# Weights times v in a sliding-window attention: four matmuls of 512 columns become six of 256, and GpSimd takes the filler's low parts

## The chip, the cores and the metric

The kernel runs on one core of a Trainium2 chip. The core has a matrix engine (TensorE, PE in the profile, with its weight loads as PEld), VectorE (DVE), ScalarE (ACT), GpSimd (POOL), a queue that issues transfers (SyncE, SP), and 16 DMA engines between HBM and the on-chip memory SBUF. [...] The metric is the device time of one execution in microseconds.

## The reference

One decoder layer at batch 1, 1,024 positions and width 1,024, in fp32. A normalised input goes through one projection to q, k, v, gates and a recurrent branch. The part that the change touches is the attention: 16 heads of 64 in four groups that share a k and a v head, a window of 128 positions, blocks of 128 queries, and a learned sink a head:

```python
diff = qi + BLOCK - kj
band = (diff >= 0) & (diff < WINDOW)          # WINDOW = BLOCK = 128
...
m = jnp.maximum(jnp.max(s, axis=-1, keepdims=True), sink)
p = jnp.exp(s - m)
denom = jnp.sum(p, axis=-1, keepdims=True) + jnp.exp(sink - m)
o = jnp.einsum('bnkgqs,bnskd->bnqkgd', p / denom, vb)
```

A query sees exactly 128 keys: those of its own block up to itself, and of the block before those behind its own offset. The attention output is gated, projected, and merged with the recurrent branch, which is projected too. An output projection, a residual and a final normalisation end the layer.

## The kernel before

Precision is kept by splitting: an operand becomes a rounded part and the rest, and a product takes three matmuls (high by high, high by low, low by high). The kernel has three large stages: the input projection with the recurrent branch, the attention with the recurrent branch's output projection as filler between its matmuls, and the closing projections. The order of every engine's queue is the order in which the program issues instructions: it is written out by hand.

Attention runs over 32 units, eight blocks for each of four groups; a unit holds four heads by 128 queries. Because exactly 128 keys count, the weights of a unit are folded into one 128 by 128 tile a head: key slot s holds the own block's key where s is at most the query's offset, else the key of the block before. So the output is the sum over all slots of the weight times v of the block before, and over the slots up to the query's offset of the weight times the difference of the two blocks of v. For each unit:

- `scores` (L1330): eight matmuls of 256 columns into the only score buffer; `maxima_a` copies the own block to `p` on ScalarE (L1339), `maxima_d` overwrites it by mask with the block before (L1345) and takes maxima (L1350) on VectorE. `sink` writes the sink's column of `p` on GpSimd (L1318).
- `weights_a`, `weights_d`: exponentials on ScalarE (L1355), division on VectorE (L1362).
- `transposed` (L1369) puts keys on the partitions; `split_a` (L1374, ScalarE) and `split_d` (L1380, VectorE) make the high part `phc` and the low part `plc`; `masks` (L1389, GpSimd) makes masked copies `phm` and `plm`.
- `values` (L1403): four matmuls of 512 columns, `phc` and `plc` by the block before, `phm` and `plm` by the difference. The first block of a group has the two unmasked ones alone. The stationary operand holds v's high part in columns 0 to 63 and its low part in 64 to 127.
- `join_a` (L1412, L1413) and `join_d` (L1423, L1424) add the two halves of the result; `a_prep` multiplies by the gate (L1538) and splits again (L1543, L1548, L1553).

In pass u of the main loop stand the scores of unit u, the weights of u - 1, the transposes and masks of u - 2 and the values of u - 3, with pieces of filler of 12 matmuls (L173). Filler operands are cast on ScalarE (L105, list `later_a`, at the end of a pass) and their rest is subtracted on VectorE (L111, list `later_d`, early in the next pass).

`v_prep` computes per group, in the projection stage, the differences and splits of v and stores both in HBM (`vd_d`). `load_v` brings, for two units at a time, the block before and the difference to `vd`, from GpSimd's queue. Steps of the projection stage are placed by a planner that adds the costs written beside them.

The tiles of attention lie in SBUF in a stack from high to low addresses: `kq1`, `yo`, `pp`, `at`, opened by `open_attn`, in space that the recurrent branch has just left. A tile waits for whatever last used its bytes. The last block of the recurrent branch is stored from `it` and `av` by GpSimd's queue (`yl_d<-it`, `yh_d<-av`). In `pp` lie three tiles `p`, of 2,064 B a partition.

Of the kernel before, what the change touches and what calls it, by code (L numbers as in the profile page):

```python
# [22 lines left out]
P = 128  # L23
# [25 lines left out]
KEEP_BUSY = 4  # L49
SLACK = 1.0, 1.3, -1.0  # L50
BANKS = (0, 1, 2, 3), (4, 5, 6, 7)


@with_exitstack
def tile_hybrid_block(ctx, tc, x, pk, rows, posr, posi, c_row, w_ss, w_gate, w_main, w_v,
# [8 lines left out]
    def f32(ap):  # L64
        return ap.bitcast(F32)
# [40 lines left out]
        else:  # L106
            A.activation(dst[0][:], src, AF.Copy, scale=scale)

    def rest(dst, src, scale=1.0):
        if scale == 1.0:  # L110
            V.tensor_tensor(out=dst[1][:], in0=src, in1=f32(dst[0][:]), op=ALU.subtract)  # L111
# [18 lines left out]
    vd_d = [tc.dram_tile([P, 8, 2, P], F32, name=f"vd_d{g}") for g in range(NG)]  # L130
# [1023 lines left out]
    def v_prep(g):  # L1154
        t = {}
        vpp = W["vpp"]

        def f0():
            t["v"] = vpp.tile([P, 8, 64], F32, tag="v32", name="v32")
            dma(t["v"][:], v_d[:, :, g, :], G)  # L1160

        def f1():
            t["d"] = vpp.tile([P, 8, 64], F32, tag="d32", name="d32")
            V.tensor_tensor(out=t["d"][:, 1:8, :], in0=t["v"][:, 1:8, :],
                            in1=t["v"][:, 0:7, :], op=ALU.subtract)
            V.tensor_copy(t["d"][:, 0, :], t["v"][:, 0, :])

        def f2():
            for n_ in ("vs", "dv"):
                t[n_] = vpp.tile([P, 8, P], F32R, tag=n_, name=n_)  # L1170
            A.copy(t["vs"][:, :, 0:64], t["v"][:])
            A.copy(t["dv"][:, :, 0:64], t["d"][:])

        def f3():
            for n_, d_ in (("v", "vs"), ("d", "dv")):
                V.tensor_tensor(out=t[d_][:, :, 64:128], in0=t[n_][:],
                                in1=f32(t[d_][:, :, 0:64]), op=ALU.subtract)
            dma(vd_d[g][:, 1:8, 1, :], t["vs"][:, 0:7, :], G)
            dma(vd_d[g][:, :, 0, :], t["dv"][:], G)

        waiting[1].extend([[("S", 0, 0, f0)], slots(6), [("D", 0, 0.85, f1)],
                           [("A", 1.24, 0, f2)], [("D", 0, 1.38, f3)]])


# [109 lines left out]
    def load_kq(m):
        g, t0 = m // 4, (m % 4) * 256
# [6 lines left out]
        dma(qs[:], q_d[g][m % 4].rearrange("(a j) t -> a j t", j=4))  # L1302
        U["kq", m] = ks, qs

    def load_v(m):
        g, n0 = m // 4, (m % 4) * 2
        vd = at.tile([P, 2, 2, P], F32R, tag="vd", name="vd", bufs=2)
        if n0:
            dma(vd[:], vd_d[g][:, n0:n0 + 2, :, :], G)
        else:  # L1310
            dma(vd[:, 0, 0, :], vd_d[g][:, 0, 0, :], G)
            dma(vd[:, 1, :, :], vd_d[g][:, 1, :, :], G)
        U["v", m] = vd

    def sink(u):
        px = U["p", u] = W["pp"].tile([P, 4, P + 1], F32, tag="p", name="p")
# [47 lines left out]

    def transposed(u):
        px = U.pop(("s", u))[1]
        pt = psx.tile([P, 4, P], F32, tag="t", name="pt")
        for j in range(4):
            W["pe"] = T.transpose(pt[:, j, :], px[:, j, 0:P], ident[:])  # L1369
        U["t", u] = [pt]  # L1370

    def split_a(u):
        phc = at.tile([P, 4, P], F32R, tag="phc", name="phc")
        A.copy(phc[:], U["t", u][0][:])  # L1374
        U["t", u].append(phc)

    def split_d(u):
        pt, phc = U.pop(("t", u))
        plc = at.tile([P, 4, P], F32R, tag="plc", name="plc")
        V.tensor_tensor(out=plc[:], in0=pt[:], in1=f32(phc[:]), op=ALU.subtract)  # L1380
        U["m", u] = phc, plc

    def masks(u):
        phc, plc = U["m", u]
        ms = []
        if u % 8:
            for s_, tag in ((phc, "phm"), (plc, "plm")):
                d_ = W["yo"].tile([P, 4, P], F32R, tag=tag, name=tag)
                G.affine_select(out=d_[:], in_=f32(s_[:]), pattern=[[0, 4], [1, P]],  # L1389
                                compare_op=ALU.is_ge, fill=0.0, base=0,  # L1390
                                channel_multiplier=-1)
                ms.append(d_)
        U["m", u] = [phc, plc], ms

    def values(u):
        n = u % 8
        vd = U["v", u // 2]
        full, masked = U.pop(("m", u))
        prods = [(vd[:, n % 2, 1 if n else 0, :], m) for m in full]
        prods += [(vd[:, n % 2, 0, :], m) for m in masked]  # L1400
        pv = psx.tile([P, 4 * P], F32, tag="v", name="pv")
        for i, (b, m) in enumerate(prods):
            W["pe"] = T.matmul(pv[:], b, m[:].rearrange("p j q -> p (j q)"),  # L1403
                               start=(i == 0), stop=(i == len(prods) - 1))
        U["pv", u] = [pv[:].rearrange("p (a e q) -> p a e q", a=2, e=2)]
        if n % 2 == 0 and u // 2 + 1 < 16:
            load_v(u // 2 + 1)

    def join_a(u):
        pvv = U["pv", u][0]  # L1410
        ob = W["yo"].tile([P, 2, P], F32, tag="ob", name="ob")
        A.copy(ob[0:64], pvv[64:128, :, 0, :])  # L1412
        A.copy(ob[64:128], pvv[0:64, :, 1, :])  # L1413
        U["pv", u].append(ob)

    def join_d(u):
        g, n = u // 8, u % 8
        pvv, ob = U.pop(("pv", u))
        if n % 2 == 0:
            W["yq"] = W["yo"].tile([P, 2, 256], F32, tag="yq", name="yq", bufs=3)  # L1420
            U["yq", u // 2] = W["yq"]
        yo = W["yq"][:, :, (n % 2) * P:(n % 2 + 1) * P]
        V.tensor_tensor(out=yo[0:64], in0=pvv[0:64, :, 0, :], in1=ob[0:64], op=ALU.add)  # L1423
        V.tensor_tensor(out=yo[64:128], in0=pvv[64:128, :, 1, :], in1=ob[64:128], op=ALU.add)  # L1424


    ps_ctx = ExitStack()
# [9 lines left out]
    def prep_r(e, i):  # L1437
        def f1():
            O[e, i] = slot()
            cast(O[e, i], R[e][i])  # L1440
        later_a.append(f1)
        later_d.append(lambda: rest(O[e, i], R[e][i]))
        if "att" not in W:
            do_later()

# [248 lines left out]
    for u in range(32 + 3):  # L1694
# [4 lines left out]
            maxima_d(u)  # L1699
        if 1 <= u < 33:  # L1700
            weights_a(u - 1)
        do_later(later_d)
        low = [steps_[2] for steps_ in high]
        while high:
            high.pop(0)[1]()
# [21 lines left out]
        if "hpool" in W:  # L1727
            for f in low:
                f()
            if late and ("gq", late[0]) in U and u >= loaded[late[0]] + 2:  # L1730
                high.append(a_prep(late.pop(0)))
                high[0][0]()
        do_later(later_a)
        if u >= 3 and u % 2 == 0:
            late.append((u - 3) // 2)
        if u >= 2 and len(loaded) < 16 and len(loaded) <= (u - 2) // 2 and (
# [323 lines left out]
```

## Time and profile before

| what | value |
|---|---|
| median of 3 runs | 907.06 us (906.17 to 907.93) |
| the profiled execution's own time | 907.17 us |
| its span, first to last instruction | 905.5 us |
| PE, DVE, ACT, POOL busy | 99%, 79%, 63%, 14% of the span |
| granted TensorE clock | 0.999 |
| HBM traffic | 199 GB/s over the span |

A row of a timeline gives start and duration in us, engine, line, operation, written tile and read tiles, shape and count; in square brackets the idle time before it and what ended it. A row of a group ends with busy us and mean ns of one, then the idle time before. A stage row gives for each engine the busy time and, in parentheses, the number of instructions. A row of waits gives the total in us, the times and the longest.

### The profile page before, as it was taken

The numbers are of one execution on the slowest core, as the hardware profiler recorded it, in microseconds if no ns is written. First come the engines' busy times: TensorE is split into PE (matmuls) and PEld (weight loads), VectorE is DVE, ScalarE is ACT, GpSimd is POOL, SyncE is SP. The second block draws the span as 40 slices with busy tenths as digits, with TensorE's granted clock in tenths as the row PEclk, the third lists the DMA queues.
The fourth block names the chain that finished last, engine by engine and source line by source line (L and its number), as shares of the span: only waits on it lengthen the run. The fifth ranks groups of instructions, "written<-read, shape, count | busy, mean of one in ns | idle before, by whom it ended". The sixth has DMA issues, their size and how long they took to land.

```text
span 905.5 us, 12654 instructions
## 1 busy us (share of the span) xinstructions
PE 895.4 (99%) x4258; PEld 746.2 (82%) x4259; DVE 717.1 (79%) x1073; ACT 567.4 (63%) x1098; POOL 124.7 (14%) x216
## 2 busy tenths in 40 slices
PE   9999999999999999999999999999999999999997
PEld 6789888888888888888888888888888888888886
DVE  6987688988669875987788597999989846578855
ACT  7965554654566855786485884888888732115535
POOL 6520251200000000000000002343443300000000
PEclk9999999999999999999999999999999999999999
DMA  9829489772435353354446367996655289416604
GB/s 355 339 69 286 164 258 319 256 235 95 151 128 180 123 209 135 125 183 162 157 144 213 105 201 242 344 401 217 214 202 203 83 306 367 140 47 232 209 1 186
DMA packets 87349, 180.74 MB, mean 200 GB/s; under 512 B 8642, under 2 KB 29138, under 8 KB 87284
## 3 DMA queue, kind: packets, MB, share of 16 engines
q1 hardware_dynamic: 83200, 167.07, 52.5%
q0 software_dynamic: 3936, 12.59, 4.4%
q8 instruction: 34, 0.56, 0.3%
q14 instruction: 31, 0.25, 0.1%
q10 hardware_dynamic: 148, 0.27, 0.1%
HBM read 121.34 MB, written 58.95 MB: 199 GB/s over the span
## 4 chain that ended last, share of the span: by engine, by line
PE 52%; issue 42%; DVE 3%; ACT 2%; DMA 1%; POOL 0%; DVEq 0%; ACTq 0%; POOLq 0%
PE rp L173 14%; PE bk L709 10%; PE out L1863 6%; PE pmain L173 5%; PE s_ps L1330 3%; PE pv L1403 3%; PE pmain L485 2%; PE bk L485 2%; PE pt L1369 1%; DMA yl_d<-it 1%; PE pmain L1579 1%; PE pmain L1580 1%; PE pmain L1578 1%; ACT jk L1881 1%; PE bk L256 1%
## 5 line engine op out<-in xcount | busy, mean ns | idle before, releaser
L709 PE MATMUL bk<-nh,wh 128*128 128x512 f32 x368 | 143.4, 390 | 0.0
L709 PE MATMUL bk<-nl,wh 128*128 128x512 f32 x368 | 143.3, 389 | 0.0
L709 PE MATMUL bk<-nh,wl 128*128 128x512 f32 x368 | 98.4, 389 | 0.0
L111 DVE TENSOR_TENSOR wl<-r,wh 128x512 fp32r<-128x512 f32 x109 | 74.8, 692 | 23.3 <-ACT wh L105 23.2
L105 ACT CAST wh<-r 128x512 fp32r<-128x512 f32 x107 | 65.6, 618 | 32.1 <-PE rp L173 11.8
L709 PEld LDWEIGHTS bk<-nh,wl 128*128 128x128 f32 x368 | 69.1, 188 | 14.3
L709 PEld LDWEIGHTS bk<-nh,wh 128*128 128x128 f32 x368 | 69.2, 188 | 14.2
L709 PEld LDWEIGHTS bk<-nl,wh 128*128 128x128 f32 x368 | 69.1, 188 | 14.1
L709 PE MATMUL bk<-hh,wh 128*128 128x512 f32 x184 | 71.7, 390 | 0.0
L709 PE MATMUL bk<-hl,wh 128*128 128x512 f32 x184 | 71.6, 389 | 0.0
L111 DVE TENSOR_TENSOR wl<-ws,wh 128x512 fp32r<-128x512 f32 x76 | 52.1, 686 | 7.2 <-ACT wh L105 7.1
L62 POOL DMA_DIRECT2D yh_d<-av x1 | 0.6, 567 | 371.9 <-ACT av L1092 371.9
L1355 ACT ACTIVATE p<-p,small 128x129 f32<-128x129 f32 x128 | 50.0, 396 | 0.0
L709 PE MATMUL bk<-hh,wl 128*128 128x512 f32 x184 | 49.2, 389 | 0.0
L105 ACT CAST wh<-ws 128x512 fp32r<-128x512 f32 x76 | 46.0, 614 | 4.8 <-DVE ws L731 2.4
L709 PEld LDWEIGHTS bk<-hh,wl 128*128 128x128 f32 x184 | 34.6, 188 | 7.1
L709 PEld LDWEIGHTS bk<-hh,wh 128*128 128x128 f32 x184 | 34.6, 188 | 7.1
L709 PEld LDWEIGHTS bk<-hl,wh 128*128 128x128 f32 x184 | 34.6, 188 | 7.1
L1330 PEld LDWEIGHTS s_ps<-ks,qs 128*128 128x128 f32 x256 | 34.1, 189 | 4.4 <-DVE p L1345 2.0
L1330 PE MATMUL s_ps<-ks,qs 128*128 128x256 f32 (+1 forms) x256 | 35.6, 282 | 0.3 <-DVE p L1345 0.2
L709 PE MATMUL bk<-hha,wh 128*128 128x512 f32 x92 | 35.8, 390 | 0.0
L709 PE MATMUL bk<-hla,wh 128*128 128x512 f32 x92 | 35.8, 389 | 0.0
(378 smaller groups left out, 2293.1 us busy)
## 6 DMA issues: line engine op xcount, KB each, us to landing
r<-w_main SPq DMA_DIRECT2D x100, 256.0 KB, 4.2
wada<-w_ss SPq DMA_DIRECT2D x16, 512.0 KB, 9.0
qs<-q_d SPq DMA_DIRECT2D x16, 512.0 KB, 5.2
wo_d<-wr SPq DMA_DIRECT2D x28, 256.0 KB, 3.1
wo<-wo_d SPq DMA_DIRECT2D x14, 512.0 KB, 5.6
ks<-k_d SPq DMA_DIRECT2D x12, 384.0 KB, 4.3
xt<-x SPq DMA_DIRECT2D x8, 512.0 KB, 7.1
sma_d<-c SPq DMA_DIRECT2D x16, 256.0 KB, 4.4
```

The lines of the kernel that those rows point to most:

```text
L105: A.copy(dst[0][:], src)
L111: V.tensor_tensor(out=dst[1][:], in0=src, in1=f32(dst[0][:]), op=ALU.subtract)
L173: mm = T.matmul(ps[hf], ww, xx[kc][hf], start=(kc == 0 and ww is w_h and xx is xh), stop=(kc == KC - 1 and xx is xl))
L256: T.matmul(bk[i % 2], zero[:, 0:P], zero, start=True, stop=True)
L485: T.matmul(starts[c][hf], ww[:, c0:c0 + P], xh[kc][hf], start=(kc == 0 and t_ == "h"), stop=(kc == KC - 1 and t_ == "l"))
L709: W["pe"] = T.matmul(ps, ww[:, kc * P:(kc + 1) * P], b[kc][i], start=(first and n == 0), stop=(n == 11), skip_group_check=not first)
L1330: W["pe"] = T.matmul(o, qs[:, j, qc], ks[:, kb:n % 2 + 2, b, :], start=(b == 0), stop=(b == 1))
L1355: A.activation(px[:, j, :], px[:, j, :], AF.Exp, bias=sm[:, 0, j:j + 1], accum_out=sm[:, 1, j:j + 1])
L1369: W["pe"] = T.transpose(pt[:, j, :], px[:, j, 0:P], ident[:])
L1403: W["pe"] = T.matmul(pv[:], b, m[:].rearrange("p j q -> p (j q)"), start=(i == 0), stop=(i == len(prods) - 1))
L1578: T.matmul(o, hh[kc][th][:, ts_], wh[:, cols], start=(kc == 0), stop=False)
L1863: T.matmul(o, a[k][x_][:, p * P:(p + 1) * P], b[k][y_][:, cols], start=(first and k == 0 and i == 0), stop=(k == 3 and i == 2), skip_group ...
```

## The change

Queries of a unit are taken in two halves. For the first 64 queries of a block the base is v of the block before, as it was; the difference, own less before, matters only for keys 0 to 63, since all later keys are of the block before. For the last 64 the base is v of the own block, and the correction, before less own, matters only for keys 64 to 127. So a correction has 64 keys, and its high and low weights are stacked on 128 partitions: per half two base matmuls and one for the correction, each of 256 columns. A block of v is loaded once, as `vb`, and serves two units; the signed differences come in pairs of units, repeated on both halves of the partitions. The masks become four selects of 64 partitions by 256 columns into one tile `pm`. Of the filler's subtractions those issued in attention go to GpSimd, behind their cast at the end of the pass.

```diff
+TOP, END = slice(0, 64), slice(64, 128)
...
-    def rest(dst, src, scale=1.0):
+    def rest(dst, src, scale=1.0, eng=V):
         if scale == 1.0:
-            V.tensor_tensor(out=dst[1][:], in0=src, in1=f32(dst[0][:]), op=ALU.subtract)
+            eng.tensor_tensor(out=dst[1][:], in0=src, in1=f32(dst[0][:]), op=ALU.subtract)
...
         def f1():
-            V.tensor_tensor(out=t["d"][:, 1:8, :], in0=t["v"][:, 1:8, :],
-                            in1=t["v"][:, 0:7, :], op=ALU.subtract)
+            for h, a, b in ((TOP, 1, 0), (END, 0, 1)):
+                V.tensor_tensor(out=t["d"][h, 1:8, :], in0=t["v"][h, a:a + 7, :],
+                                in1=t["v"][h, b:b + 7, :], op=ALU.subtract)
...
-            dma(vd_d[g][:, 1:8, 1, :], t["vs"][:, 0:7, :], G)
-            dma(vd_d[g][:, :, 0, :], t["dv"][:], G)
-        waiting[1].extend([[("S", 0, 0, f0)], slots(6), [("D", 0, 0.85, f1)],
+            dma(vs_d[g], t["vs"][:], G)
+            for l, half_ in enumerate((TOP, END)):
+                dma(dv_d[g][:, :, l, :], t["dv"][half_, :, :], G)
+        waiting[1].extend([[("S", 0, 0, f0)], slots(6), [("D", 0, 1.4, f1)],
...
         load_v(0)
+        load_d(0)
+        load_v(1)
...
+    def load_v(u):
+        vb = U["v", u] = at.tile([P, P], F32R, tag="vb", name="vb", bufs=4)
+        dma(vb[:], vs_d[u // 8][:, u % 8, :], G)
+
+    def load_d(m):
+        n0 = m % 4 * 2
+        vd = U["d", m] = at.tile([P, 2, 2, P], F32R, tag="vd", name="vd", bufs=2)
+        dma(vd[:], dv_d[m // 4][:, n0:n0 + 2, :, :].unsqueeze(0).to_broadcast([2, 64, 2, 2, P]), G)
...
-        pt = psx.tile([P, 4, P], F32, tag="t", name="pt")
+        pt = psx.tile([P, 2, 4, 64], F32, tag="t", name="pt")
...
     def masks(u):
         phc, plc = U["m", u]
-        ms = []
         if u % 8:
-            for s_, tag in ((phc, "phm"), (plc, "plm")):
-                d_ = W["yo"].tile([P, 4, P], F32R, tag=tag, name=tag)
-                G.affine_select(out=d_[:], in_=f32(s_[:]), pattern=[[0, 4], [1, P]],
-                                compare_op=ALU.is_ge, fill=0.0, base=0,
-                                channel_multiplier=-1)
+            pm = W["yo"].tile([P, HALF], F32R, tag="pm", name="pm")
+            lo, hi = slice(0, 256), slice(256, HALF)
+            for to, s_, from_, cols in ((TOP, phc, TOP, lo), (END, phc, END, hi),
+                                        (END, plc, TOP, lo), (TOP, plc, END, hi)):
+                d = 1 if cols is lo else -1
+                G.affine_select(out=pm[to, cols], in_=f32(s_[from_, cols]),
+                                pattern=[[0, 4], [d, 64]], compare_op=ALU.is_ge, fill=0.0,
+                                base=min(d, 0), channel_multiplier=-d)
+            U["m", u] = phc, plc, pm
...
     def values(u):
         n = u % 8
-        vd = U["v", u // 2]
-        full, masked = U.pop(("m", u))
-        prods = [(vd[:, n % 2, 1 if n else 0, :], m) for m in full]
-        prods += [(vd[:, n % 2, 0, :], m) for m in masked]
+        m = U.pop(("m", u))
+        base = [U.pop(("v", u - 1)), U["v", u]] if n else [U["v", u]]
         pv = psx.tile([P, 4 * P], F32, tag="v", name="pv")
-        for i, (b, m) in enumerate(prods):
-            W["pe"] = T.matmul(pv[:], b, m[:].rearrange("p j q -> p (j q)"),
-                               start=(i == 0), stop=(i == len(prods) - 1))
+        for l, vb in enumerate(base):
+            cols = slice(l * 256, l * 256 + 256) if n else slice(0, HALF)
+            for i, t_ in enumerate(m):
+                w = vb[:] if i < 2 else U["d", u // 2][:, n % 2, l, :]
+                W["pe"] = T.matmul(pv[:, cols], w, t_[:, cols],
+                                   start=(i == 0), stop=(i == len(m) - 1))
         if n % 2 == 0 and u // 2 + 1 < 16:
-            load_v(u // 2 + 1)
+            load_d(u // 2 + 1)
+        U["pv", u] = [pv[:].rearrange("p (l a e q) -> p l a e q", l=2, a=2, e=2)]
+        if u + 2 < 32:
+            load_v(u + 2)
...
-        later_d.append(lambda: rest(O[e, i], R[e][i]))
+        later_d.append(lambda: rest(O[e, i], R[e][i], eng=G if "att" in W else V))
...
             weights_a(u - 1)
-        do_later(later_d)
...
-        do_later(later_a)
+        do_later()
```

`split_a`, `split_d`, `join_a` and `join_d` follow the new order of columns (half, head, query) with the same numbers of elements.

More of the change, by code (lines that the diff above doesn't have):

```diff
@@ L129, in tile_hybrid_block @@
     v_d = tc.dram_tile([P, 8, NG, 64], F32, name="v_d")
-    vd_d = [tc.dram_tile([P, 8, 2, P], F32, name=f"vd_d{g}") for g in range(NG)]
+    vs_d = [tc.dram_tile([P, 8, P], F32, name=f"vs_d{g}") for g in range(NG)]
+    dv_d = [tc.dram_tile([64, 8, 2, P], F32, name=f"dv_d{g}") for g in range(NG)]
     q_d = [tc.dram_tile([4, 512, 256], F32, name=f"q_d{g}") for g in range(NG)]
@@ L1303, in load_kq @@
         U["kq", m] = ks, qs
[L1305 to L1313, printed above, removed]
+    def load_v(u):
[5 more added lines that the diff above has]
+        dma(vd[:], dv_d[m // 4][:, n0:n0 + 2, :, :].unsqueeze(0).to_broadcast([2, 64, 2, 2, P]), G)
     def sink(u):
@@ L1366, in transposed @@
         px = U.pop(("s", u))[1]
-        pt = psx.tile([P, 4, P], F32, tag="t", name="pt")
+        pt = psx.tile([P, 2, 4, 64], F32, tag="t", name="pt")
         for j in range(4):
-            W["pe"] = T.transpose(pt[:, j, :], px[:, j, 0:P], ident[:])
-        U["t", u] = [pt]
+            W["pe"] = T.transpose(pt[:, :, j, :], px[:, j, 0:P], ident[:])
+        U["t", u] = [pt[:].rearrange("p l j q -> p (l j q)")]
     def split_a(u):
-        phc = at.tile([P, 4, P], F32R, tag="phc", name="phc")
-        A.copy(phc[:], U["t", u][0][:])
+        phc = at.tile([P, HALF], F32R, tag="phc", name="phc")
+        A.copy(phc[:], U["t", u][0])
         U["t", u].append(phc)
@@ L1378, in split_d @@
         pt, phc = U.pop(("t", u))
-        plc = at.tile([P, 4, P], F32R, tag="plc", name="plc")
-        V.tensor_tensor(out=plc[:], in0=pt[:], in1=f32(phc[:]), op=ALU.subtract)
+        plc = at.tile([P, HALF], F32R, tag="plc", name="plc")
+        V.tensor_tensor(out=plc[:], in0=pt, in1=f32(phc[:]), op=ALU.subtract)
         U["m", u] = phc, plc
@@ L1384, in masks @@
         phc, plc = U["m", u]
-        ms = []
         if u % 8:
-            for s_, tag in ((phc, "phm"), (plc, "plm")):
-                d_ = W["yo"].tile([P, 4, P], F32R, tag=tag, name=tag)
-                G.affine_select(out=d_[:], in_=f32(s_[:]), pattern=[[0, 4], [1, P]],
-                                compare_op=ALU.is_ge, fill=0.0, base=0,
-                                channel_multiplier=-1)
-                ms.append(d_)
-        U["m", u] = [phc, plc], ms
+            pm = W["yo"].tile([P, HALF], F32R, tag="pm", name="pm")
@@ L1405, in values @@
-        U["pv", u] = [pv[:].rearrange("p (a e q) -> p a e q", a=2, e=2)]
+        for l, vb in enumerate(base):
[4 more added lines that the diff above has]
+                                   start=(i == 0), stop=(i == len(m) - 1))
         if n % 2 == 0 and u // 2 + 1 < 16:
-            load_v(u // 2 + 1)
+            load_d(u // 2 + 1)
@@ L1409, in join_a @@
+        U["pv", u] = [pv[:].rearrange("p (l a e q) -> p l a e q", l=2, a=2, e=2)]
+        if u + 2 < 32:
+            load_v(u + 2)
     def join_a(u):
         pvv = U["pv", u][0]
-        ob = W["yo"].tile([P, 2, P], F32, tag="ob", name="ob")
-        A.copy(ob[0:64], pvv[64:128, :, 0, :])
-        A.copy(ob[64:128], pvv[0:64, :, 1, :])
+        ob = W["yo"].tile([P, 2, 2, 64], F32, tag="ob", name="ob")
+        A.copy(ob[0:64], pvv[64:128, :, :, 0, :])
+        A.copy(ob[64:128], pvv[0:64, :, :, 1, :])
@@ L1421, in join_d @@
             U["yq", u // 2] = W["yq"]
-        yo = W["yq"][:, :, (n % 2) * P:(n % 2 + 1) * P]
-        V.tensor_tensor(out=yo[0:64], in0=pvv[0:64, :, 0, :], in1=ob[0:64], op=ALU.add)
-        V.tensor_tensor(out=yo[64:128], in0=pvv[64:128, :, 1, :], in1=ob[64:128], op=ALU.add)
+        yo = W["yq"][:, :, (n % 2) * P:(n % 2 + 1) * P].rearrange("p a (l q) -> p l a q", l=2)
+        V.tensor_tensor(out=yo[0:64], in0=pvv[0:64, :, :, 0, :], in1=ob[0:64], op=ALU.add)
+        V.tensor_tensor(out=yo[64:128], in0=pvv[64:128, :, :, 1, :], in1=ob[64:128], op=ALU.add)
     ps_ctx = ExitStack()
```

## The prediction

> **What bounds the kernel now.** I read four views, from coarse to fine: the busy shares of the page, the stages by time, one attention unit on TensorE in order of time, and what TensorE's weight loads waited for.
>
> ```profile
> PE 895.4 (99%) x4258; PEld 746.2 (82%) x4259; DVE 717.1 (79%) x1073; ACT 567.4 (63%) x1098; POOL 124.7 (14%) x216
> ...
> core 0: us, PE busy (x) PEld busy (x) DVE busy (x) ACT busy (x) POOL busy (x), PEclk, DMA share, GB/s
> 60.00:540.00 480.00, 480.00 (x2210) 401.80 (x2209) 384.06 (x521) 305.86 (x452) 25.92 (x40) 1.00 0.54 179
> ...
> 574.00:731.00 157.00, 156.91 (x855) 133.44 (x854) 140.05 (x258) 127.18 (x399) 60.70 (x108) 1.00 0.64 229
> 731.00:905.00 174.00, 167.99 (x752) 139.32 (x751) 114.72 (x162) 64.06 (x112) 0.00 (x0) 1.00 0.51 188
> ```
> TensorE (PE) never rests before 731 us, so a microsecond of matmuls taken out of the attention stage (574 to 731) comes off the end, unless another engine takes over. VectorE (DVE), 140.05 of 157 us busy there, is the one that could; GpSimd (POOL) has 60.70.
>
> ```profile
> 649.15 0.60 PE L1369 MATMUL pt<-ident,p 128*128 128x128 f32 x4
> 649.51 0.48 PE L1403 MATMUL pv<-phc,vd 128*128 128x512 f32 x1
> 649.82 0.40 PE L1403 MATMUL pv<-plc,vd 128*128 128x512 f32 x1
> 650.05 0.40 PE L1403 MATMUL pv<-phm,vd 128*128 128x512 f32 x1
> 650.29 0.40 PE L1403 MATMUL pv<-plm,vd 128*128 128x512 f32 x1
> 650.52 1.10 PE L1330 MATMUL s_ps<-ks,qs 128*128 128x256 f32 x8
> 651.47 0.63 PE L173 MATMUL rp<-yh,wh 128*128 128x512 f32 x2
> ...
> 654.22 0.60 PE L1369 MATMUL pt<-ident,p 128*128 128x128 f32 x4
> ...
> PEld s_ps L1330 <- DVE p L1345: 2.0, 5, 0.7
> ```
> One unit lasts 654.22 - 649.15 = 5.07 us with no gap. Its parts, from start to start: transposes 0.36, weights times v 1.01, scores 0.95, filler 2.75. The only waits are five of the scores on VectorE, 2.0 us in all: VectorE is already close behind.
>
> **The change, part by part.**
>
> **Weights times v.** In 28 of 32 units (the first of each group of eight keeps its two matmuls) four matmuls of 512 columns become six of 256. The last three of the four start 0.23 apart (649.82 to 650.52: 0.70 for three), so the four cost 4 x 0.233 = 0.93 beside a lead of 0.08 before the second, which stays. A matmul of 256 columns with a weight load of its own stands in the same unit: the eight scores take 651.47 - 650.52 = 0.95, or 0.119 each. Six cost 0.71. Saved: 0.22 x 28 = **6.1 us**. The bounds: at half of 0.233 each the six cost 0.70 (6.4 us saved); if a change of weights cost them more than it costs the scores, at most 0.155 each would save nothing. I take 0.119, the same type and shape.
>
> **New waits of TensorE.** The six read `vb`, `vd` and `pm`, which come from two DMAs and GpSimd. Queued behind such a wait are the rest of the values, the next scores and the filler. Nothing, if the producers are early; up to the 0.08 of the lead for one more wait in each of 28 units, 2.2 us. I take 0.5, as the data lie ready a unit ahead.
>
> **The opening of attention.** Tiles of `pp` lie below `yo`, and `yo` shrinks by 2,048 B a partition, since `pm` takes the place of `phm` and `plm`. So `p` moves up by that much, and `at` grows by it (`vb`) beneath.
>
> ```profile
> 554.00 0.55 POOL L62 DMA_DIRECT2D yl_d<-it  x1 [1.81 <-DVE it L1096]
> 555.62 1.73 POOL L1318 COPY p<-pk_t 128x4 f32<-128x4 f32 x1
> 558.94 0.59 ACT L1339 COPY p<-s_ps 128x512 f32<-128x512 f32 x1 [2.38 <-PE s_ps L1330]
> 561.51 1.11 PE L1330 MATMUL s_ps<-ks,qs 128*128 128x256 f32 x8
> 562.42 0.31 POOL L1318 COPY p<-pk_t 128x4 f32<-128x4 f32 x2 [2.18 <-DMA yl_d<-it]
> 565.62 1.21 PE L1330 MATMUL s_ps<-ks,qs 128*128 128x256 f32 x8 [0.24 <-DVE p L1345]
> ...
> DMA to landing us min/median/max: 8.3/8.3/8.3
> ```
> The store `yl_d<-it` lands 8.3 us after 554.00. The second and third `p` tiles lie on `it` and wait for it (562.42); the first, free at 555.62, ends 1,232 B below `it` by the sizes of the tiles, and after the shift overlaps it by 816 B. Then ScalarE's first copy of scores, today at 558.94, waits until about 562.4 and ends at 563.0; the single score buffer is held, and the second scores, today at 561.51, start at 563.05. Behind the copy on ScalarE wait a cast and a bank's copy of the filler. TensorE loses **1.5 us**, and 0.1 after it, as VectorE's row comes later by about as much. Bounds: 0, if the store lands before 558.94, and 3 us, if the filler's bank waits too. I take 1.6.
>
> **The filler's low parts on GpSimd, and the masks.**
>
> ```profile
> L111 DVE TENSOR_TENSOR wl<-r,wh 128x512 fp32r<-128x512 f32 x18 | 12.5, 693 | 0.0
> L1389 POOL TENSOR_SCALAR_AFFINE_SELECT plm<-plc 128x512 fp32r<-128x512 f32 x28 | 17.7, 632 | 15.0 <-DVE plc L1380 14.4 <-PE s_ps L1330 0.6
> L589 POOL TENSOR_SCALAR_AFFINE_SELECT mf<-mf 128x128 f32<-128x128 f32 x1 | 0.4, 390 | 0.1
> L297 POOL TENSOR_TENSOR a<-a,t 128x64 f32<-128x64 f32 x2 | 0.6, 318 | 0.2
> L351 POOL TENSOR_TENSOR trn<-trn,r 128x128 f32<-128x128 f32 x1 | 0.6, 578 | 0.1
> L62 POOL DMA_DIRECT2D vd<-vd_d x20 | 11.0, 553 | 2.3 <-PE pv L1403 2.0 <-issue 0.3
> ...
> 600.79 0.64 POOL L1389 TENSOR_SCALAR_AFFINE_SELECT phm<-phc 128x512 fp32r<-128x512 f32 x1 [1.16 <-ACT phc L1374]
> 600.91 1.07 DVE L1362 TENSOR_TENSOR p<-p,small 128x512 f32<-128x512 f32 x1
> ...
> 622.14 0.68 DVE L1380 TENSOR_TENSOR plc<-pt,phc 128x512 fp32r<-128x512 f32 x1
> 626.61 0.69 DVE L1380 TENSOR_TENSOR plc<-pt,phc 128x512 fp32r<-128x512 f32 x1
> ...
> 645.68 0.69 DVE L1380 TENSOR_TENSOR plc<-pt,phc 128x512 fp32r<-128x512 f32 x1 [0.29 <-PE pv L1403]
> 646.51 0.63 POOL L1389 TENSOR_SCALAR_AFFINE_SELECT plm<-plc 128x512 fp32r<-128x512 f32 x1 [0.21 <-DVE plc L1380]
> 647.36 0.69 DVE L1538 TENSOR_TENSOR yq<-yq,r 128x512 f32<-128x512 f32 x1
> ```
> VectorE loses up to 18 subtractions, 12.5 us, two in every four units. Without one its round is 626.61 - 622.14 = 4.47 us, against a new unit of 5.07 - 0.22 = 4.85.
>
> GpSimd gets them. No row has the subtraction at 512 wide. From 0.318 at 64 wide to 0.578 at 128 is 4.1 ns a column, which gives 2.1 us at 512; at the 2.1 ns that remain if the second had waited half its extra, 1.25 us; the floor is the 0.632 of a one-input pass. I take 1.25, nearer the select's own slope, (632 - 390)/384 = 0.6 ns, than 4.1. [...]
>
> The four selects of 64 partitions by 256 are between 0.39 and 0.63 each; I take 0.45, so 1.8 us a unit where it was 1.26. Loads rise from 20 to 48 (32 `vb`, 16 `vd`), 28 x 0.553 = 15.5 us of issue on POOL. POOL sums, over 157 us: 60.7 + 28 x 0.5 + 18 x 1.25 + 15.5 = 113. Behind a subtraction waiting for its cast stand the next loads, the sink column and the next masks. The last of them is due at the third matmul of the next unit's values: plm was due by 650.05 and ended at 647.14, 2.9 us early; 0.6 longer masks and 1.25 of subtraction leave about 1.
>
> The price is elsewhere: at 600.91 a VectorE pass with two SBUF operands ran 1.07 instead of 0.69 because a GpSimd pass had begun 0.12 us before; it stood for what was left of that, less 0.14. The multiply at 647.36 comes 1.68 after `plc`; the new subtraction can start when two last masks are done, 0.83 + 0.9 after `plc`: a tie. If GpSimd is first, VectorE loses up to 1.25 - 0.14 = 1.1 us; four units then hold 4 x 4.47 + 2 x 1.1 = 20.1 against 4 x 4.85 = 19.4 of TensorE. At half of the cases it is 19.0, and VectorE keeps up, with a late copy here and there: 1.0 us in all. Against it stand the scores' waits that the relief removes, of 2.0 us about 0.7 outside the opening. Net +0.3; bounds -0.7 and +6.
>
> **Hidden.** In preparation of v, one subtraction becomes two on 64 partitions, and two stores become three, in the stage 60 to 540, where PE is busy 480.00 of 480 and DVE 384.06. The cover gone, four times one more pass of about 0.69 would be 3 us. `rest` now runs right behind its cast, half a unit earlier than on VectorE; its reader comes units later. The layout of transposes and joins changes no element count: 0.
>
> **The sum.** -6.1 + 0.5 + 1.6 + 0.3 = -3.7. The profiled execution took 907.17 (span 905.5), 0.11 over the median 907.06: 907.17 - 3.7 = 903.5, as a median **903.4 us**.
>
> **The rivals.**
>
> **All of the gain.** The store lands early or the tile isn't held, and no lock bites: 907.06 - 6.1 + 0.5 - 0.7 = 900.8. For it: the first `p` clears `it` by few bytes either way; against it: the 8.3 us of landing.
>
> **VectorE takes the gain.** GpSimd is always first, at 1.25: seven groups of four units from 593 on, where the multiplies begin, at 20.1 instead of 19.4, leave 7 x 0.7 = 4.9 lost: the 1.0 above becomes 4.9, and 903.4 + 3.9 = 907.3, no change.
>
> [...] If the subtraction takes 1.7 us, the middle of 1.25 and 2.1, and always begins before the multiply, VectorE stands 1.55 twice in four units: 4 x 4.47 + 3.1 = 21.0 against the 20.3 of before. Seven times 0.7, with 1.6 at the opening and 0.9 of gain where no multiplies run: 907.06 + 4.9 + 1.6 - 0.9 = 912.7. It decides from a subtraction of about 1.4 us on. For it: 600.91. Against it: a VectorE already late starts its multiply behind a lock less often, since the masks wait for the same `plc`. [...]
>
> **It doesn't do what it says.** The six matmuls come at 0.155, bound by their weight loads: 907.06 + 1.6 + 0.3 = 909.0. The scores' 0.119 speak against it.
>
> **How the numbers follow.** The forecast has 0.52 (its own range 901.5 to 905.5), all of the gain 0.17, VectorE 0.16, the lock 0.10, no gain in matmuls 0.05. A measurement of this kernel can tell about 0.2%, 1.8 us, from no change. Faster by more: 0.17 and nearly all of the forecast, 0.66. Within: the rest of it and most of VectorE's case, 0.20. Slower: 0.14. Range 900.0 to 909.0: it leaves out the lock and a little below.
>
> **What would show it.** `pv` rows of 256 columns, 0.12 apart, and a unit of 4.85 us; the first `p` copy of ScalarE waiting for `yl_d<-it`, with the second scores near 563; the subtraction's mean on POOL near 1.25; VectorE's multiplies lengthened in some units, not in all. The prediction is wrong if units last 5 us or more, if scores wait for VectorE in most units, or if values wait for `pm`.

## The result, and the profile after

| | before | after |
|---|---|---|
| median | 906.71 us (906.17 to 907.93) | 917.12 us (916.15 to 917.89) |
| ratio, 95% interval | | 1.0112 (1.0095 to 1.013) |
| span of the profiled execution | 905.5 us | 915.5 us |
| granted TensorE clock, mean | 0.999 | 0.992 |

The kernel became 10.4 us slower where 3.7 us of gain were forecast. The stages of after, in the same columns as those of before (the attention stage in three pieces), say where it was lost.

```profile
core 0: us, PE busy (x) PEld busy (x) DVE busy (x) ACT busy (x) POOL busy (x), PEclk, DMA share, GB/s
574.00:600.00 26.00, 24.88 (x145) 20.89 (x143) 21.41 (x40) 21.87 (x69) 18.70 (x38) 1.00 1.03 327
600.00:640.00 40.00, 35.61 (x194) 30.51 (x195) 29.93 (x53) 26.61 (x87) 22.35 (x42) 0.91 0.91 288
640.00:731.00 91.00, 89.47 (x533) 77.57 (x532) 80.88 (x143) 76.67 (x242) 65.21 (x121) 1.00 0.60 190
```

TensorE, which stood still for 0.1 us of this stage before, now stands still for 1.12 + 4.39 + 1.53 = 7.0 us. VectorE is less busy than it was (132.2 of 157 us, 140.1 before), so it isn't the new bound. In 600 to 640 the granted clock is 0.91 as well. The waits of TensorE in after (total in us, times, longest) name the releaser:

```profile
PE pv L1410 <- DMA vd<-dv_d: 5.5, 6, 3.5
PE rp L175 <- DMA yl<-yl_d: 0.8, 1, 0.8
PE rp L175 <- DMA yh<-yh_d: 0.6, 1, 0.6
```

The load of the signed differences, `vd<-dv_d`, is what the third of the six matmuls waits for. The worst case and what follows it, TensorE in order of time:

```profile
607.53 0.60 PE L1374 MATMUL pt<-ident,p 128*128 128x128 f32 x4
607.89 0.36 PE L1410 MATMUL pv<-phc,vb 128*128 128x256 f32 x1
608.09 0.28 PE L1410 MATMUL pv<-plc,vb 128*128 128x256 f32 x1
611.83 0.55 PE L1410 MATMUL pv<-pm,vd 128*128 128x256 f32 x1 [3.46 <-DMA vd<-dv_d]
...
614.66 1.05 PE L175 MATMUL rp<-yh,wh 128*128 128x512 f32 x2
615.52 1.05 PE L175 MATMUL rp<-yh,wl 128*128 128x512 f32 x2
616.37 1.05 PE L175 MATMUL rp<-yl,wh 128*128 128x512 f32 x2
...
618.98 0.60 PE L1374 MATMUL pt<-ident,p 128*128 128x128 f32 x4
```

And the stage rows of the same stretch:

```profile
613.00:615.00 2.00, 2.00 (x10) 2.00 (x10) 1.48 (x3) 1.23 (x4) 1.33 (x4) 0.50 1.07 241
615.00:617.00 2.00, 2.00 (x6) 1.52 (x5) 1.83 (x4) 2.00 (x10) 0.82 (x2) 0.50 1.05 334
```

This unit takes 618.98 - 607.53 = 11.45 us instead of 4.85. The wait itself is 3.46 us. Behind it two filler matmuls take 615.52 - 614.66 = 0.86 us instead of 0.46, and the stage rows give the reason: the granted clock (the third number from the end) is 0.50. So one late load costs 3.5 us of waiting and some 3 us of half speed.

How late the loads are stands in the transfers of 560 to 740 us. First those of before, then those of after (count, KB each, median us from issue to landing):

```profile
q0 software_dynamic: 1697, 5.31, 8.4%
...
r<-ga_d SPq DMA_DIRECT2D x16, 256.0 KB, 4.6
...
vd<-vd_d POOLq DMA_DIRECT2D x12, 256.0 KB, 5.2
yh<-yh_d SPq DMA_DIRECT2D x6, 512.0 KB, 9.5
```
```profile
q0 software_dynamic: 9928, 7.89, 15.5%
...
r<-ga_d SPq DMA_DIRECT2D x16, 256.0 KB, 7.5
...
vd<-dv_d POOLq DMA_DIRECT2D x15, 256.0 KB, 10.3
yh<-yh_d SPq DMA_DIRECT2D x6, 512.0 KB, 13.3
...
vb<-vs_d POOLq DMA_DIRECT2D x30, 64.0 KB, 8.7
```

The load has the same 256 KB as its forerunner and takes twice as long. It is issued two units, 9.7 us, ahead of its reader, so a landing of 10.3 us in the middle comes too late for many of them; TensorE waits for six. Its neighbours are late too. GpSimd's queue, q0, carries 9,928 packets instead of 1,697.

The matmuls themselves came as forecast. An undisturbed unit of after:

```profile
648.29 0.60 PE L1374 MATMUL pt<-ident,p 128*128 128x128 f32 x4
648.65 0.36 PE L1410 MATMUL pv<-phc,vb 128*128 128x256 f32 x1
648.85 0.28 PE L1410 MATMUL pv<-plc,vb 128*128 128x256 f32 x1
648.97 0.28 PE L1410 MATMUL pv<-pm,vd 128*128 128x256 f32 x1
649.08 0.28 PE L1410 MATMUL pv<-phc,vb 128*128 128x256 f32 x1
649.20 0.28 PE L1410 MATMUL pv<-plc,vb 128*128 128x256 f32 x1
649.32 0.28 PE L1410 MATMUL pv<-pm,vd 128*128 128x256 f32 x1
649.44 1.12 PE L1335 MATMUL s_ps<-ks,qs 128*128 128x256 f32 x8
```

The second to the sixth start 0.12 apart, and the values take 649.44 - 648.65 = 0.79 instead of 1.01: 0.22 saved.

**Where the 10.4 us come from.** From the second scores to the 32nd, after falls from 1.52 us behind before to 9.80 behind: 8.3 us. The values of 24 masked units stand between, so 24 x 0.22 = 5.3 us of gain were due there, and 13.6 us went astray: 7.0 of standing still, and some 3.1 of clock (half speed from the end of the wait at 611.83 to about 618). Most of the other 3.5 stands behind the waits, which cost more than the idle time in their rows. The unit between the scores at 580.61 and those at 586.52, for example, lasts 5.91 us, 1.06 more than 4.85, with 0.38 us of idle time before its third matmul: behind it the values start 0.31 and 0.22 apart instead of 0.12, and the scores start 0.33 behind the last of them. Some 0.8 remain in the best version below as well, where their place can be seen.

### The profile page after: what moved, and what is told of

It is laid out like the page before. It is cut to its first block, busy times and chain, and to the rows that moved or that the text cites. A ratio compares the mean times of both kernels' runs of the same rounds, so it can differ in the third digit from the quotient of the medians.

```text
span 915.5 us, 12836 instructions
## 1 busy us (share of the span) xinstructions
PE 898.2 (98%) x4315; PEld 749.5 (82%) x4315; DVE 713.7 (78%) x1059; ACT 568.2 (62%) x1098; POOL 173.9 (19%) x322
## 2 busy tenths in 40 slices
DMA packets 95670, 183.42 MB, mean 200 GB/s; under 512 B 16323, under 2 KB 36819, under 8 KB 95605
## 3 DMA queue, kind: packets, MB, share of 16 engines
q0 software_dynamic: 12256, 15.28, 5.9%
## 4 chain that ended last, share of the span: by engine, by line
issue 41%; PE 38%; DMA 10%; DVE 6%; ACT 3%; POOL 1%; POOLq 0%; DVEq 0%; ACTq 0%
PE rp L175 11%; DMA vd<-dv_d 7%; PE bk L711 6%; PE out L1871 4%; PE pmain L175 4%; PE bk L487 3%; PE pmain L487 2%; PE s_ps L1335 2%; PE pv L1410 2%; DMA wo<-wo_d 1%; PE pmain L1588 1%; PE pmain L1587 1%; PE pmain L1589 1%; DMA yl_d<-it 1%; PE pt L1374 1%
## 5 line engine op out<-in xcount | busy, mean ns | idle before, releaser
L112 DVE TENSOR_TENSOR wl<-r,wh 128x512 fp32r<-128x512 f32 x91 | 62.1, 690 | 23.3 <-ACT wh L106 23.1
L112 DVE TENSOR_TENSOR wl<-ws,wh 128x512 fp32r<-128x512 f32 x76 | 52.1, 685 | 11.4 <-ACT wh L106 11.3
L1379 ACT CAST phc<-pt 128x512 fp32r<-128x512 f32 x32 | 18.7, 585 | 31.9 <-PE pv L1410 16.3
```

Of the source, the lines that this page charges most:

```text
L112: eng.tensor_tensor(out=dst[1][:], in0=src, in1=f32(dst[0][:]), op=ALU.subtract)
L1379: A.copy(phc[:], U["t", u][0])
```

## The experiments

The 907.06 us of the first table of before is the median of three runs, and 906.71 that of four, these three among them. Three theories stood at first. **A:** the repeated source of the load cuts it into many short packets (the packet count of q0), and they delay it and its neighbours. **B:** it is the bytes, since each pair of units reads its differences twice. **C:** the load is a side show, and GpSimd's subtractions shut VectorE out. A fourth, **D**, came from the packet records later. Times of before are 906.6, 907.0, 907.3 and 906.7 us in the four groups of runs.

### The differences stored twice, loaded plainly (dup)

```diff
-    dv_d = [tc.dram_tile([64, 8, 2, P], F32, name=f"dv_d{g}") for g in range(NG)]
+    dv_d = [tc.dram_tile([P, 8, 2, P], F32, name=f"dv_d{g}") for g in range(NG)]
...
-                dma(dv_d[g][:, :, l, :], t["dv"][half_, :, :], G)
+                for to in (TOP, END):
+                    dma(dv_d[g][to, :, l, :], t["dv"][half_, :, :], G)
...
-        dma(vd[:], dv_d[m // 4][:, n0:n0 + 2, :, :].unsqueeze(0).to_broadcast([2, 64, 2, 2, P]), G)
+        dma(vd[:], dv_d[m // 4][:, n0:n0 + 2, :, :], G)
```

> The changed kernel, with the signed differences stored twice in HBM, once for each half of the partitions, so that the load of a pair of units is one plain transfer of 128 rows of 2 KB, as the load of before was, and not a broadcast of 64 rows. Theory A (the broadcast load is cut into short packets, lands after 10.5 us where the load of before took 5.2, and TensorE waits for it): vd lands in 5 to 6 us, no matmul of the values waits for it, the granted clock stays at 1.0 in the window from 600 to 640 us, units last 4.85 us, time 901 to 903 us. Theory B (too many bytes and loads in the stretch in which the DMA engines are full, whatever their shape): vd still takes 8 us or more and TensorE still waits, 910 to 917 us. Theory C (VectorE shut out by GpSimd's subtractions): no change, 915 to 918 us.

907.53 us (ratio 1.0014, 1.0005 to 1.0023): 9.6 us faster than after, but not the 901 to 903 of theory A, and still not faster than before. The load lands in 5.8 us in the middle, and no wait for it is left. Between the second and the 32nd scores 4.15 us are gained, but attention starts some 5 us late. They are lost in the projection stage. The stages of this kernel there, and then, in order of time, what GpSimd, VectorE and TensorE did:

```profile
140.00:160.00 20.00, 18.02 (x80) 14.61 (x79) 12.35 (x18) 8.13 (x16) 4.06 (x6) 1.00 0.92 261
160.00:180.00 20.00, 20.00 (x83) 16.21 (x82) 18.62 (x30) 11.14 (x20) 4.05 (x6) 0.91 0.84 253
```
```profile
141.66 2.71 POOL L63 DMA_DIRECT2D dv_d<-dv  x4
...
157.34 1.28 DVE L1210 SCALAR_TENSOR_TENSOR gate_bc<-wr,pk_t,gate_bc 128x1024 f32<-128x1024 f32 x1 [6.61 <-DMA wr<-w_gate]
158.54 0.68 DVE L114 SCALAR_TENSOR_TENSOR wl<-ws,wh 128x512 fp32r<-128x512 f32 x1
...
159.28 1.21 PE L711 MATMUL bk<-nh,wl 128*128 128x512 f32 x4 [1.98 <-DVE wl L114]
```

Four stores of 256 KB go out at 141.66. A row of gate weights lands late, VectorE stands 6.61 us in front of it, the subtraction that TensorE needs (`wl`) stands behind it on VectorE, and TensorE waits 1.98 us, after which the clock falls again (0.91 over the next 20 us). The same stretch of before is full, with a clock of 1.00. That the two added stores delayed the row is the reading of these lines; the version with a later copy, below, bears it out.

### The repeated load from SyncE's queue (sp)

```diff
-        dma(vd[:], dv_d[m // 4][:, n0:n0 + 2, :, :].unsqueeze(0).to_broadcast([2, 64, 2, 2, P]), G)
+        dma(vd[:], dv_d[m // 4][:, n0:n0 + 2, :, :].unsqueeze(0).to_broadcast([2, 64, 2, 2, P]))
```

> The changed kernel, with the broadcast load of the differences issued from SyncE's queue in place of GpSimd's; its shape stays. If the short packets are the cause (theory A), it still takes 9 us or more to land, and the waits stay: 912 to 918 us. If GpSimd's own writing of the transfer is the cause, it lands in 5 to 6 us and the time is 901 to 904 us.

936.98 us (1.0328, 1.0311 to 1.0345), much worse than the 912 to 918 of theory A. TensorE's first wait in this kernel:

```profile
PE pv L1410 <- DMA vd<-dv_d: 21.6, 7, 7.7
```

GpSimd's queue alone isn't the cause: with the same shape on the other queue TensorE waits 21.6 us for the load, against 5.5 in after. I took it for A. It wasn't: q0 falls from 12,256 packets over the execution to 3,808, yet the packets counted under 512 B in the whole execution are 8,930 here, against 16,323 in after and 8,642 before. The short packets were gone, and TensorE waited longer for the load than ever. I only saw this when D was formed.

### The lock: low parts back on VectorE (dup_v), and on GpSimd in the kernel before (before_g)

`dup_v` is `dup` with the filler's subtractions back on VectorE, at the places of before. `before_g` is the kernel before with only these subtractions moved.

```diff
-        later_d.append(lambda: rest(O[e, i], R[e][i]))
+        later_d.append(lambda: rest(O[e, i], R[e][i], eng=G if "att" in W else V))
...
-        do_later(later_d)
...
-        do_later(later_a)
+        do_later()
```

> The kernel with the differences stored twice, and the filler's low parts back on VectorE early in the next pass, as before. Theory A: VectorE has 4 x 4.47 + 2 x 0.6 = 19.1 us of work in four units of 19.4, so the time is that of the run with the differences stored twice alone, within 1.5 us. Theory C: faster than that run by 5 us or more.

> The kernel before, with only the filler's low parts issued in attention moved to GpSimd, behind their cast. Theory A: the few waits of the scores for VectorE (2.0 us in all) go and some new ones come, 906 to 907.5 us, no change. Theory C: 912 us or more.

The lock can be read from the rows of before: of the VectorE passes `p<-p,small` and `yq<-yq,r` between 574 and 690 us, the four that begin while a GpSimd pass has 0.3 us or more to run take 0.91 to 1.11 us instead of 0.69 (at 595.39, 600.91, 616.02 and 637.63). What holds them no run shows.

908.43 us (1.0020, 1.0011 to 1.003) and 906.74 us (1.0002, 0.9993 to 1.0012). C falls: alone, the move makes no difference that can be told, and with the rest of the change it is worth at most the 0.9 us between `dup` and `dup_v`, whose intervals overlap. TensorE's weight loads for the scores wait for VectorE's rows 1.1 us in `before_g`, 2.0 before.

### Two plain loads of 64 partitions (two)

The same bytes are read twice, from a store as in after, but in two transfers.

```diff
-        dma(vd[:], dv_d[m // 4][:, n0:n0 + 2, :, :].unsqueeze(0).to_broadcast([2, 64, 2, 2, P]), G)
+        for h in (TOP, END):
+            dma(vd[h, :, :, :], dv_d[m // 4][:, n0:n0 + 2, :, :], G)
```

> The differences are stored as in the changed kernel; each pair of units loads them with two plain transfers of 64 partitions in place of one with a repeated source. If the shape of the load is the cause (its 8,400 short packets, theory A): the difference lands in about 6 us, TensorE's waits for it vanish, the attention stage keeps its gain of 4.2 us, and since the projection stage stores no more than the changed kernel does, nothing is lost there: 902 to 904 us. If reading the differences twice, in whatever shape, is what the queue can't bear (theory B): waits for vd of some us remain and the time is above 908 us.

905.83 us (0.9988, 0.998 to 0.9997): 11.3 us faster than after by a change of the load alone, so B falls, though the 902 to 904 expected are missed. Each half lands in 5.6 us. The gain between the second and the 32nd scores is only 1.98 us. One filler matmul of `two` shows where 1.0 of it went:

```profile
618.70 0.73 PE L175 MATMUL rp<-yl,wh 128*128 128x512 f32 x2 [0.98 <-DMA yl<-yl_d]
```

`yl` lands in 11.7 us here, in 9.9 before.

### More lead for the load (early, early2, two_early)

`early` keeps the repeated load and issues it one unit sooner; `two_early` does the same to the two plain loads.

```diff
-        if n % 2 == 0 and u // 2 + 1 < 16:
-            load_d(u // 2 + 1)
+        if n % 2 and u // 2 + 2 < 16:
+            load_d(u // 2 + 2)
```

> The repeated-source load stays, but it is issued one unit earlier (behind the values of the odd unit that frees its buffer), so it has about 14.6 us in place of 9.7 before its reader. If TensorE's loss is the load being late (it lands in 10.5 us in the middle): waits for vd vanish, the granted clock stays at 1.00 from 574 to 640, the short waits for yh and yl (1.4 us) remain: 904 to 906 us. If the short packets harm by crowding the DMA engines, whoever waits: the other loads stay late, TensorE waits for yh and yl instead, and the time is 910 us or more.

> Both edits: plain loads, issued a unit earlier. If the plain load lands in about 6 us it is early enough without the second edit, and the time is that of the plain load alone within 0.7 us. If 9.7 us are still too short for some of the loads, it is faster than the plain load alone by 1 us or more.

949.64 us (1.0474, 1.0457 to 1.049) and 907.47 us (1.0007, 0.9998 to 1.0015): both misses, and by my own edit. Both kernels also load the second pair at the opening, as does `early2`. In `early`, GpSimd's first wait and TensorE's:

```profile
POOL vd L63 <- PE pv L1411: 55.7, 14, 7.0
```
```profile
PE pv L1411 <- DMA vb<-vs_d: 27.9, 10, 5.9
```

The buffer comes free with the values of the very unit behind which the load is now issued, so GpSimd stands in front of it, fourteen times (in `two_early` twelve times, 21.2 us in all); behind it on GpSimd stand `vb` and the masks of the same pass, and TensorE waits for `vb`. `early2` puts the load at the end of the pass, behind `vb` and the masks:

```diff
             masks(u - 2)
+        if u >= 3 and u % 2 == 0 and (u - 3) // 2 + 2 < 16:
+            load_d((u - 3) // 2 + 2)
```

> The repeated-source load stays. It is issued about 13 us before its reader, at the end of the pass, behind the masks and behind the load of vb, so GpSimd doesn't stand before it. If TensorE lost its time because this load came late: no waits for vd, clock 1.00 from 574 to 640, 903 to 907 us. If its short packets crowd the DMA engines: vb, yl or yh come late instead, and the time stays above 909 us.

921.24 us (1.0156, 1.0143 to 1.017). Its waits:

```profile
PE pv L1411 <- DMA vb<-vs_d: 8.0, 2, 6.5
PE pv L1411 <- DMA vd<-dv_d: 4.6, 1, 4.6
```

Lead doesn't mend it. The load lands in 11.7 us and the transfer behind it in the same queue, `vb`, is late in its place.

### Theory D: two DMA engines out of sixteen

The packet records of the traces say what the repeated load is made of. GpSimd's queue between 560 and 740 us, packets by size:

```
            4096 B   8 B (mean us each: 0.009)
before        1297      0
after         1912   7168
two           1799      0
late          1841      0
gap           1920   7168
```

7,168 is 16 times 448: each of the 16 loads brings 448 packets of 8 B. The 256 KB themselves go in 64 packets of 4 KB, as ever. So the "short packets" carry 3.5 KB a load, and their times add up to 4 us. What stands out is how the 64 run. From one load of after, their starts (us, from the first shown, at 639.31) and durations (ns):

```
0.000 173    0.022 171
0.169 168    0.189 173
0.334 171    0.358 168
0.501 171    0.523 171
0.668 173    0.690 171
```

They come two at a time, a pair every 0.167 us, and so on for 20 pairs. So it would look if two engines each worked through 32 packets, one packet behind the other, 32 x 0.168 = 5.4 us when nothing else is on them; and 448 is 32 for each of the other 14. Between 575 and 640 us 3.0 packets of 4 KB of this queue are in flight on the mean, when any is, in after, and 6.0 in `two`. By that reading anything else that had a share on those two engines would wait in line, which fits the late `vb`, `yh` and `r` (medians of 8.7, 13.3 and 7.5 us in after; 4.8 in `two`, and 9.5 and 4.6 before). The source here begins with a 2, which fits as well. No record names an engine, so their number is an estimate of the author's from these counts.

What remained was whether it is the leading 2 or the repetition. `gap` has no repetition: the second copy lies in HBM, one row too far for the two blocks to be one dimension of 128.

### The copy made later (late), and the same with a gap (gap)

`late` is `dup` with one store, and the second copy made from HBM to HBM, placed in the program late in the recurrent branch. GpSimd seems to have issued these four copies sooner, between 140 and 200 us: it has 15 instructions there in `late` (11 in `two`), and none from 200 to 540. The DMA share is 0.84 in the first of these stretches and 0.47 in the second. `gap` differs from it in the second copy's place alone.

```diff
+    for g in range(NG):
+        at_slot(7 * (len(pairs) - N_ATT) - 60 + 8 * g, ("N", 0, 0, lambda g=g: dma(
+            dv_d[g][END, :, :, :], dv_d[g][TOP, :, :, :], G)))
```
```diff
-    dv_d = [tc.dram_tile([P, 8, 2, P], F32, name=f"dv_d{g}") for g in range(NG)]
+    dv_d = [tc.dram_tile([130, 8, 2, P], F32, name=f"dv_d{g}") for g in range(NG)]
...
-        dma(vd[:], dv_d[m // 4][:, n0:n0 + 2, :, :], G)
+        dma(vd[:], dv_d[m // 4].rearrange("(h p) n l c -> h p n l c", h=2)[:, 0:64, n0:n0 + 2, :, :], G)
...
-            dv_d[g][END, :, :, :], dv_d[g][TOP, :, :, :], G)))
+            dv_d[g][65:129, :, :, :], dv_d[g][TOP, :, :, :], G)))
```

> The differences lie twice in HBM, so that a pair of units is loaded in one plain transfer of 128 partitions, but the second copy is made from the first, from HBM to HBM, some 60 to 36 steps of filler before attention, where the DMA engines are under half busy. If the doubled stores of the projection stage made VectorE wait for a gate row and TensorE behind it (theory A): no wait between 140 and 200 us, attention starts where it did before, within 1 us, and the stage's gain of 4.1 us comes off the end: 902 to 903.5 us. If attention's gain is given back in the stages behind it: 905 us or more, as with the two half transfers.

> As in the kernel with the late second copy, but that copy lies one row further (row 65 on), so the load reads two blocks of 64 rows that can't be taken as one of 128: no row is read twice, and the leading dimension of the source has size 2. If the leading 2 is the cause (theory D: the data of such a load go through 2 of the 16 DMA engines; in the changed kernel its 4 KB packets come two at a time, 0.17 us each, 64 of them in 5.4 us): the load again shows 448 packets of 8 B beside 64 of 4 KB, lands in 9 us or more, TensorE waits for vd, and the time is 910 to 918 us. If reading a row twice in one transfer is the cause: it lands in about 6 us and the time is that of the contiguous copy, about 904 us.

`late`: 904.09 us (0.9968, 0.9955 to 0.998), 0.6 above the range expected. `gap`: 918.17 us (1.0162, 1.0101 to 1.0222; one of its runs took 928.57). One row of distance, and 14 us. TensorE's first wait in `gap`, the landing of its load by the view of the tile `vd` (lowest, median, highest), and the same of `late`:

```profile
PE pv L1410 <- DMA vd<-dv_d: 6.7, 4, 2.3
```
```profile
DMA to landing us min/median/max: 8.5/10.8/16.7
```
```profile
DMA to landing us min/median/max: 2.9/5.6/6.6
```

The leading dimension of 2 is shown to be the cause: it suffices, with nothing read twice. That it means two engines rests on the packet records alone, and was not shown. In `late`, TensorE is full from 140 to 200 us and the first scores start 0.1 us ahead of those of before, the second 0.7 behind, so the start that `dup` lost is back; from the second scores to the 32nd it gains 4.33 us.

### p above yo (two_swap, late_swap)

```diff
-        W["yo"] = pool(at_ctx, "yo", side="right")
         W["pp"] = pool(at_ctx, "pp", bufs=3, side="right")
         W["pp"].tile([P, 72], F32, name="pad", bufs=1)
+        W["yo"] = pool(at_ctx, "yo", side="right")
```

> Plain loads, and the tiles of p are opened above those of yo, so that none of the three lies on the store's tile it. If the opening costs what the two traces show (the second scores 1.5 us later, of which 0.8 is a later start): the second scores start about 1 us earlier and the time is 0.5 to 1.5 us under that of the plain loads alone. If the wait moves to another tile of the stack: no change.

> The same, with p opened above yo. The wait of the second scores for ScalarE's copy (0.5 us) vanishes: 0.3 to 0.8 us under the one without it, or nothing, if the wait for VectorE's rows of the third scores grows by as much.

905.38 us (0.9982, 0.9973 to 0.999) and **903.32 us** (0.9957, 0.9943 to 0.9971): 0.5 and 0.8 us under their partners, with overlapping intervals, so the size isn't settled. That the wait for ScalarE's copy is gone is seen: `late` has it (0.7 us, once), `late_swap` not. `late_swap` is the best of all, 3.9 us faster than before (by its ratio, 2.6 to 5.2) and 13.8 faster than after. Its attention stage, and what its weight loads wait for:

```profile
574.00:600.00 26.00, 26.00 (x164) 23.12 (x163) 22.96 (x41) 22.00 (x70) 21.52 (x41) 1.00 0.99 367
600.00:640.00 40.00, 39.48 (x239) 34.42 (x238) 36.38 (x67) 35.16 (x111) 30.27 (x56) 1.00 0.80 293
640.00:731.00 91.00, 90.94 (x531) 78.90 (x531) 78.37 (x142) 72.33 (x222) 59.22 (x111) 1.00 0.57 196
```
```profile
PEld s_ps L1335 <- DVE p L1350: 2.1, 4, 0.7
```
```profile
613.63 1.02 PEld L1335 LDWEIGHTS s_ps<-ks,qs 128*128 128x128 f32 x8 [0.47 <-DVE p L1350]
```

TensorE is full but for 0.6 us, at a clock of 1.00, and its weight loads still wait for VectorE. Here stand the 0.8 us: in the three later units whose values are the two matmuls of a group's first block, the scores follow each other in 4.80 us instead of 4.60, held by such a wait, and the unit behind each saves 0.12 instead of 0.22.

Not all of what attention saves reaches the end. At about 730 us `late_swap` is 4.9 us ahead of before, and at the end 3.9. The rest goes in one place of the closing stage:

```profile
837.56 0.73 PE L1874 MATMUL out<-wo,mh 128*128 128x512 f32 x2 [0.63 <-ACT out L1919]
```

ScalarE's copy stands there behind two casts of `wo`, which wait for the loads `wo<-wo_d` and run only 3.9 us earlier than in the kernel before. TensorE waits for the same copy 0.6 us in after, `two` and `late`, and not in before. Why these loads don't move up by the whole 4.9 was not followed up.

## Why the prediction was wrong, step by step

**Weights times v: right.** Forecast 0.22 a unit at 0.119 a matmul; 0.22 and 0.12 measured. The gain of 6.1 us was there to be had: with the load mended, `late_swap` keeps 4.5 of the 5.3 due between the second scores and the 32nd.

**New waits of TensorE: the step that failed.** It said that the data lie ready a unit ahead, and took 0.5 us of at most 2.2. For `vb` in `late` that holds; for `vd` it never was worked out. The load was counted by its issue on GpSimd alone, 0.553 us, and its landing taken over unspoken from the load of before, 5.3 us. Its shape had changed in the diff: a source that begins with a 2. It landed in 10.5 us against 9.7 of lead, TensorE waited 5.5 us for it, and 1.4 for loads beside it; the clock behind the longest wait added some 3.1. The upper bound of 2.2 assumed that a wait is short. No rival had a late load; the four all argued from engines, and none from the transfers. The issue itself was a hint after the fact: 0.83 us for one such load instead of 0.553.

**The opening: right in place, smaller.** The second scores start at 563.03 as forecast, waiting for ScalarE's copy, which waits for the store:

```profile
562.39 0.59 ACT L1344 COPY p<-s_ps 128x512 f32<-128x512 f32 x1 [5.07 <-DMA yl_d<-it]
563.03 1.21 PE L1335 MATMUL s_ps<-ks,qs 128*128 128x256 f32 x8 [0.52 <-ACT p L1344]
```

But the first scores of this execution were already 0.84 us later than those of before, so the wait costs 0.5 to 0.7, not 1.6.

**Low parts and masks: right in size, and the lock is minor.** The groups of after on GpSimd:

```profile
L1396 POOL TENSOR_SCALAR_AFFINE_SELECT pm<-phc 64x256 fp32r<-64x256 f32 x56 | 26.9, 480 | 24.7 <-ACT phc L1379 22.7
L112 POOL TENSOR_TENSOR wl<-r,wh 128x512 fp32r<-128x512 f32 x17 | 24.5, 1444 | 8.5 <-ACT wh L106 7.0 <-POOL pm L1396 0.4
L1396 POOL TENSOR_SCALAR_AFFINE_SELECT pm<-plc 64x256 fp32r<-64x256 f32 x56 | 23.9, 427 | 5.4 <-ACT rp L1493 1.2 <-DVE plc L1385 0.9
```

The selects have 0.48 and 0.43 us against 0.45, the subtraction 1.44 against 1.25 (1.29 at 648.00, where VectorE stood idle from 647.63 to 649.90). Forecast net +0.3; `before_g` and `dup_v` put it between a gain of 0.9 and nothing. VectorE does get held: the low part of the gated output (`al`) takes 989 ns on the mean instead of 727, and 1.66 us at 622.44, behind a subtraction that began 0.19 before it. But VectorE had the time, with 12.5 us taken off it. So the rival of the lock (912.7 us) falls, though the subtraction passed the 1.4 us from which it was to decide: it assumed that every subtraction starts ahead of the multiply (`yq`), and the multiply takes 749 ns on the mean where it took 718.

**Hidden: right for after, by little.** Three stores and two subtractions cost TensorE nothing between 140 and 200 us of after (60.00 of 60 busy). Two more stores, in `dup`, cost some 5 us at the start of attention. "Hidden" was argued from engines that had time, while what came late in `dup` was a transfer, `wr<-w_gate`, for which VectorE stood 6.61 us.

**The rivals.** "All of the gain" would have needed the mended load, and even with it 903.3 came out, not 900.8: VectorE's waits keep 0.8 us, and 1.0 is lost in the closing stage, where the prediction let every microsecond out of attention come off the end. The rest isn't put down to rows. "VectorE takes the gain" isn't seen, and neither are matmuls at 0.155.

## What to carry to other kernels

Work out the landing of every load whose access pattern changes, not its issue alone: read the outermost dimension of its source, and where that is as small as the 2 of this case, split the load or, better here (904.1 us against 905.8), lay the data out so that the partitions lead. A load's lead is counted in its reader's units and set against the landing time in that stage (here 9.7 us against 10.3 in the middle). When a load is issued earlier, see first which wait it brings onto its queue: in `early` GpSimd stood 55.7 us in front of a buffer that came free late, and TensorE 27.9 in front of the `vb` loads queued behind it.

## What the runs showed of the hardware that was not expected

**A leading dimension of 2.** In the attention stage a 256 KB load with a leading dimension of 2 took 10.5 us in the middle to land in after and 10.8 in `gap`; a plain one of the same size took 5.6 in `late` and 5.3 before. The DMA share was 1.03, 0.91 and 0.60 in the three pieces of the stage in after, and 1.04, 0.79 and 0.57 in `late`. Issued from SyncE's queue (`sp`), the same load made the kernel slower still (936.98 us against 917.12); why it is worse there was not shown, as no view here names the engine.

**Waits of TensorE, and a clock of 0.50.** TensorE's waits of 1.98 us (`dup`), 2.34 (`gap`), 3.46 (after), 4.63 and 6.51 (`early2`) each go with a stretch of some 3.4 or 6.8 us at a granted clock of 0.50, which begins in the wait or within 2 us of its end. Behind those of 0.98 (`two`), 1.44 (`early2`) and 1.75 (`gap`) the clock stays at 1.00. The length of one wait doesn't decide it: behind 2.12 us in `sp` the filler matmuls start 0.46 apart, as at a clock of 1.00, while in `dup_v` TensorE stood still for 1.81 us in all between 140 and 200 us with a mean clock of 0.97 there, and `two_early` has 0.96 between 600 and 640, with no wait above 0.7 us. In the record of the clock in the trace of after, the changes between 1.00 and 0.50 from 24.1 us on lie 3.41, 583.7, 6.83 and 293.5 us apart, 1, 171, 2 and 86 times 3.413, so where a wait falls between such steps may matter; no run varies that alone, and what sets the clock was not shown.
